# Turned tiles through DRAM: from SyncE's queue to ScalarE's in the input projection

## Chip, cores and metric

One core of a Trainium2 chip. The metric is the device time of one execution in microseconds (us). TensorE multiplies, VectorE (DVE), ScalarE (ACT) and GpSimd (POOL) do the rest, and transfers between SBUF and DRAM are issued by SyncE (SP) or ScalarE, each from its own instruction stream onto its own DMA queue.

## The reference

One layer of a hybrid decoder, for 256 positions and 2048 channels, all in float32:

```
h = rmsnorm(x);  proj = h @ w_in                      # 2048 x 14368
q, k, v, z, b, a, p_in, g_a, g_b = split(proj)
q, k, v = silu(causal_dwconv(q, k, v))                # width 4
o = gated_delta_rule(l2norm(q), l2norm(k), v, g, beta)   # 16 heads of 128
y_a = rmsnorm(o) * silu(z)
y_b = (multi-scale causal pooling of p_in) @ pool_w * pool_scale   # 4 groups
x = x + (sigmoid(g_a) * y_a + sigmoid(g_b) * y_b) @ w_out
gate, up = split(rmsnorm(x) @ w_up)                   # 2 x 5632
x = x + (gelu(causal_dwconv(gate) + bias) * up) @ w_down
return rmsnorm(x)
```

## The kernel before

**Products.** Every weight is read once, in 512 KB tiles of 256 rows by 512 columns. SyncE loads a tile (`raw`, five buffers), ScalarE rounds it to the fast float32 format (`whi`), and VectorE makes the rest (`wlo = raw - whi`). Activations are split in the same way, and each product is three matmuls: eight with `whi` and four with `wlo` for a weight tile, each over 512 columns. The steps `fetch`, `cast` and `split` run ahead of the products, the cast by up to `AHEAD` = 3 tiles. A product leaves positions on partitions and 512 channels along the row.

**Turned tiles.** Convolution, pooling and the next product want channels on partitions. A tile is turned in three steps, in `flip`: VectorE transposes 32 x 32 blocks into `tn`; four DMAs of 128 KB (one for each 32 partitions, in runs of 32 values) write it to DRAM so that the blocks change places (`flip<-tn`); after that has landed one DMA of 512 KB reads it back in rows (`flipped`: `kq<-flip`, `vT<-flip`, `pu<-flip`, `mlo<-flip` in the input projection, `fhl<-flip`, `gs<-flip`, `us<-flip` after it). `flip_back` does the same in the other direction for the values of the delta rule (`back<-tb`, then `vt<-back`).

**Stages.** The input projection runs in four turns (g = 0 to 3) of 512 channels of q, k and v, with the pooling input and gates of the turn before between them. A turn has five flips (keys, queries, values, pooling input, mixed result) and one `flip_back`. Beside the products run the convolutions, the delta rule of four heads (`gdn`, with its own small transfers `cdd`, `lb`, `tbd`, `tct`, `qnd`, `pnt` and the decays `dec`, all on SyncE), pooling (`pooled`) and gates. Then follow the output projection (`residual`, four flips) and the gated MLP (`gated_linear`, `product`, 22 flips), and the down projection.

**Order.** Each engine runs its instructions in the order in which the program writes them. That order is made when the kernel is built: the side work is written as generators (`spawn`), each of which yields the engine that its next piece needs; `side` writes a piece out between two groups of matmuls when a model of the times (`Plan`) says that its inputs are there and its engine isn't too far ahead of TensorE. `Plan.dma` is the model of a transfer: one queue for all of them, 0.42 us of the issuer's time on SyncE and 0.1 us on ScalarE. `pipeline` chooses between `fetch`, `cast` and `split` and goes before the side work of ordinary rank. All five engines' streams follow from the same model, so a change to the model can move any of them.

An instruction that has to wait for a semaphore holds back all that stands behind it in its engine's stream: on SyncE the weight loads, on ScalarE the casts.

Of the kernel before, what the change touches and what calls it, by code (L numbers as in the profile page):

```python
# [13 lines left out]
P = 128  # L14
S = 256
# [16 lines left out]
class Plan:  # L32
# [4 lines left out]
    def __init__(self):  # L37
        self.t = dict(PE=0.0, V=0.0, A=0.0, G=0.0, S=0.0)
        self.ready = self.base = 0.0
        self.queue = 2.5  # L40
        self.table = "s"

    def at(self, time):
# [6 lines left out]
    def dma(self, eng, out):  # L50
        n = 4
        for d in out.shape:
            n *= d
        self.t[eng] = max(self.t[eng], self.base) + (0.42 if eng == "S" else 0.1)
        self.queue = max(self.queue, self.t[eng]) + n / (170e3 if out.shape[-1] <= 32 else 380e3)
        self.ready = max(self.ready, self.queue + 2.0)

    def op(self, eng, name, out, args, kw):
        if name == "dma_start":
# [48 lines left out]
def kernel(  # L108
# [20 lines left out]
    plan = Plan()  # L129
    now = plan.t  # L130
    nc = Engines(plan, tc.nc)
# [12 lines left out]
    def nm(s):  # L144
        cnt[0] += 1
        return f"{s}_{cnt[0]}"
# [32 lines left out]
    def take(*tags):  # L179
        while taken_by(tags):  # L180
            yield
        held.update((tag, 1e9) for tag in tags)
# [7 lines left out]
    def give(*tags):  # L190
        held.update((tag, plan.ready) for tag in tags)
# [25 lines left out]
    def spawn(gen, rank=1):  # L217
        cnt[0] += 1
        threads.append([rank, cnt[0], gen, None, plan.ready])
        follow(threads[-1], next(gen))  # L220
# [152 lines left out]
        return ps  # L373


    def flip(pool, src, of, rank):
        yield "V", -2
        yield from take("tn")
        b = pool.tile([P, 2, 512], F32, tag="tn", name=nm("tn"))
        if of is None:  # L380
            for t in range(2):
                nc.vector.transpose(b[:, t, :], src[:, t, :])
        else:
            nc.vector.transpose(b.rearrange("p t f -> p (t f)"), src.rearrange("p t f -> p (t f)"))
            give(of)
        yield "S"
        d = dpool.tile([512, S], F32, tag="flip", bufs=4, name=nm("flip"))
        dv = d.rearrange("(f i) (t a j) -> a i t f j", i=32, t=2, j=32)
        for a in range(4):
            nc.sync.dma_start(dv[a], b[32 * a : 32 * a + 32].rearrange("p t (f j) -> p t f j", j=32))  # L390
        give("tn")
        yield "S", rank
        return d

    def flipped(dst, d):
        nc.sync.dma_start(dst, d.rearrange("(f p) s -> p f s", p=P))

    def flip_back(pool, src, dst, of):
        yield "V"
        yield from take("tn")  # L400
        b = pool.tile([P, 4, S], F32, tag="tn", name=nm("tb"))
        nc.vector.transpose(b.rearrange("p h s -> p (h s)"), src.rearrange("p h s -> p (h s)"))
        give(of)
        yield "S"
        d = dpool.tile([S, 512], F32, tag="back", name=nm("back"))
        dv = d.rearrange("(n i) (h a j) -> a i h n j", i=32, h=4, j=32)
        for a in range(4):
            nc.sync.dma_start(dv[a], b[32 * a : 32 * a + 32].rearrange("p h (n j) -> p h n j", j=32))
        give("tn")
        yield "S"  # L410
        nc.sync.dma_start(dst.rearrange("p t h d -> p t (h d)"), d.rearrange("(t p) c -> p t c", p=P))

    mix = tc.tile_pool(name="mix", bufs=1)
    mp = mix.__enter__()
# [533 lines left out]

    def pooled(e, g, phi, plo):
        d = yield from flip(mp, e, "ev", g)  # L950
        win = WINDOWS[g]
        spare = g + 5 if g < 3 else 0
        if g == 3:
            yield from take("tn")
        u = mtile(g, [P, 4, S], F32, nm("pu"))
        flipped(u, d)
        yield "V"
        a = mtile(spare, [P, 4, S], F32, nm("pa")) if spare else mp.tile([P, 4, S], F32, tag="tn", name=nm("pa"))
# [105 lines left out]
    for g in range(4):  # L1064
# [5 lines left out]
        def keys(e, g=g, done=done):  # L1070
            d = yield from flip(mp, e, "ev", g)
            yield from take("k", "q")
            kq = mp.tile([P, 4, 2, S], F32, tag="kq", bufs=1, name=nm("kq"))
            done.append(kq)
            yield from conv_silu(d, 1, g, kq[:, :, 0, :])
            done.append(plan.ready)
# [80 lines left out]
    fp = ctx.enter_context(tc.tile_pool(name="ffn", bufs=1))  # L1157
# [13 lines left out]
    def residual(c, ps):  # L1171
        yield "V"
        xs = xt[:, :, c * 512 : (c + 1) * 512]
        if c == 2:
            for t in range(2):
                nc.vector.tensor_tensor(xs[:, t, :], xs[:, t, :], ps[:, t, :], op=ALU.add)
        else:
            nc.vector.tensor_tensor(xs, xs, ps, op=ALU.add)
        spawn(squares(c, xs), 0)
        d = yield from flip(fp, xs, None, 0)  # L1180
        ks = slice(4 * c, 4 * c + 4)
        raw = flo[:, ks, :].bitcast(F32)
        flipped(raw, d)
        for k in range(4 * c, 4 * c + 4):
            if k % 2 == 0:
                yield "A"
            nc.scalar.activation(fhi[:, k, :], raw[:, k - 4 * c, :], AF.Copy, scale=vec[:, V_FFN + k : V_FFN + k + 1])
        for k in range(4 * c, 4 * c + 4):
            if k % 2 == 0:
                yield "V"  # L1190
            nc.vector.scalar_tensor_tensor(flo[:, k, :], raw[:, k - 4 * c, :], vec[:, V_FFN + k : V_FFN + k + 1],
                                           fhi[:, k, :].bitcast(F32), op0=ALU.mult, op1=ALU.subtract)
        high.append(c)

    def squares(c, xs):
        yield "A"
        for t in range(2):
            jk = cpool.tile([P, 512], F32, tag="sqj", name=nm("sqj"))
            nc.scalar.activation(jk, xs[:, t, :], AF.Square, accum_out=ssq4[:, t, c : c + 1])
        squared.append(c)  # L1200
        if len(squared) == 4:
            yield "V"
            nc.vector.tensor_reduce(ssq2, ssq4, axis=mybir.AxisListType.X, op=ALU.add)
            rstd(ssq2, rs2)
            squared.append(4)
# [28 lines left out]
    hlo = []  # L1234

    def gated_linear(c, e, done):
        d = yield from flip(fp, e, "fev", 1)
        yield from take("gs")
        gs = fp.tile([P, 4, S], F32, tag="gs", name=nm("gs"))
        flipped(gs, d)  # L1240
        yield "V"
        yield from take("y")
        y = fp.tile([P, 4, S], F32, tag="y", name=nm("y"))
        for f in range(4):
            yield "V"
            r = 4 * c + f
            nc.vector.tensor_scalar(y[:, f, :], gs[:, f, :], cfw[:, 2 * KF + r : 2 * KF + r + 1],
                                    vec[:, V_CB + r : V_CB + r + 1], op0=ALU.mult, op1=ALU.add)
            for j in (1, 0):
                s = 2 - j  # L1250
                nc.vector.scalar_tensor_tensor(y[:, f, s:], gs[:, f, : S - s], cfw[:, j * KF + r : j * KF + r + 1],
                                               y[:, f, s:], op0=ALU.mult, op1=ALU.add)
        give("gs")
        yield "A"
        nc.scalar.activation(y, y, AF.Gelu)
        done.append((y, plan.ready))

    def product(c, e, hh, hl, done):
        d = yield from flip(fp, e, "fev", 1)
        yield from take("gs")  # L1260
        us = fp.tile([P, 4, S], F32, tag="gs", name=nm("us"))
        flipped(us, d)
        while not done:
            yield
        y, ready = done[0]
        plan.at(max(plan.ready, ready))
        yield "V"
        nc.vector.tensor_tensor(y, us, y, op=ALU.mult)
        give("gs")
        yield "A"  # L1270
        nc.scalar.copy(hh, y)
        yield "V"
        nc.vector.tensor_tensor(hl, y, hh.bitcast(F32), op=ALU.subtract)
        give("y")
# [3 lines left out]
    def up_product(c):  # L1278
        return evicted(gemm_a(fh, fl, KD, range(6, 8), first.pop(0), fh_made) if c == 0 else gemm_a(fh, fl, KD))

    for c in range(DFF // 512):
        e = up_product(c)
        done = []
        spawn(gated_linear(c, e, done))
        e = up_product(c)
        if c < 4:
            hh = mtile(c, [P, 4, S], F32R, f"hhi{c}")
            hl = mtile(4 + c, [P, 4, S], F32R, f"hlo{c}")
        else:
            hh = fp.tile([P, 4, S], F32R, name=f"hhi{c}")  # L1290
            hl = fp.tile([P, 4, S], F32R, name=f"hlo{c}")
        spawn(product(c, e, hh, hl, done))
        hhi.append(hh)
        hlo.append(hl)
# [94 lines left out]
    xs = xt[:, 1, 1536:2048]  # L1389
# [36 lines left out]
```

## Time and profile before

| | |
|---|---|
| time, median of 3 runs | 1534.53 us (1532.87 to 1534.91) |
| the profiled execution | 1536.53 us, its span 1533.5 us |
| TensorE | busy 1519.9 us, 99% of the span |
| VectorE, ScalarE | busy 1059.4 us (69%), 775.4 us (51%) |
| DMA queue of SyncE | 339.32 MB, 75.3% of the 16 DMA engines' time |
| DMA queue of ScalarE | 5.53 MB, 1.1% |

The span is the time from the first to the last instruction. PE is TensorE's matmul stream, PEld its weight loads, and SPq and ACTq are the DMA-issuing instructions of SyncE and ScalarE, which don't count as busy time. Matmul ends are modelled, so a busy TensorE isn't one at its peak; the granted clock (PEclk, 1.00 is full speed) stands beside it. Nearly all instructions have line L94, that of a helper, so groups are told apart by the tiles that they write and read, as `out<-in`. "A <- B" in a list of waits means that A sat idle until B was done; the columns are us in total, times, and the longest. For transfers, "landing" is the time from the issue to the data's arrival.

### The profile page before, as it was taken

How to read it: one execution, taken by the hardware profiler on the slowest of the kernel's cores; microseconds unless marked ns; L12 is line 12 of the kernel's file. 1: busy time of each engine (PE TensorE's matmuls, PEld its weight loads, DVE VectorE, ACT ScalarE, POOL GpSimd, SP SyncE). 2: the span in 40 equal slices, each digit the busy share in tenths (PEclk: the TensorE clock that was granted, in tenths of full speed). 3: DMA queues.
4: the chain of work that ended last, by engine and by line, in shares of the span. 5: the costliest groups of instructions: out<-in, count | busy, mean ns of one | idle time of the engine just before them, and what ended most of it. 6: DMA issues, size and time to landing. Idle time of an engine off the chain costs nothing.

```text
span 1533.5 us, 19655 instructions
## 1 busy us (share of the span) xinstructions
PE 1519.9 (99%) x7110; PEld 1250.0 (82%) x7110; DVE 1059.4 (69%) x1525; ACT 775.4 (51%) x1023; POOL 62.5 (4%) x85
## 2 busy tenths in 40 slices
PE   9999999999999999999999999999999999999997
PEld 8887888777878887888888888888888888888886
DVE  5767878787887779885566766666666666444445
ACT  7475474466545854464455544444454444333343
POOL 1001001100010002000000000000000000000000
PEclk9999999999999999999999999999999999999999
DMA  8888975898578966974798888877887788666663
GB/s 292 224 238 219 256 243 149 206 260 256 159 178 245 288 201 167 264 230 143 228 281 270 235 255 245 258 220 242 253 248 227 237 255 240 204 193 192 220 194 108
DMA packets 399271, 346.09 MB, mean 226 GB/s; under 512 B 231190, under 2 KB 258374, under 8 KB 399174
## 3 DMA queue, kind: packets, MB, share of 16 engines
q1 hardware_dynamic: 395744, 339.32, 75.3%
q10 hardware_dynamic: 3430, 5.53, 1.1%
q8 instruction: 55, 0.90, 0.2%
q14 instruction: 42, 0.34, 0.1%
HBM read 315.40 MB, written 29.39 MB: 225 GB/s over the span
## 4 chain that ended last, share of the span: by engine, by line
PE 93%; DMA 3%; DVE 2%; issue 1%; SPq 0%; ACT 0%; POOLq 0%; POOL 0%; ACTq 0%; DVEq 0%
PE psm L94 79%; PE psa L94 8%; PE psb L94 6%; DMA raw<-in_w_in_dram 2%; DVE wlo L94 1%; DMA lb<-cdd 0%; DMA pu<-flip 0%; SPq L94 0%; DVE tmp L94 0%; ACT whi L94 0%; DVE tb L94 0%; DMA flip<-tn 0%; ACT xt L94 0%; DVE pb L94 0%; DVE tn L94 0%
## 5 line engine op out<-in xcount | busy, mean ns | idle before, releaser
L94 DVE TENSOR_TENSOR wlo<-raw,whi 128x1024 fp32r<-128x1024 f32 x524 | 635.2, 1220 | 293.1 <-ACT whi L94 291.4
L94 ACT CAST whi<-raw 128x1024 fp32r<-128x1024 f32 x526 | 549.0, 1051 | 536.9 <-PE psm L94 360.7
L94 PE MATMUL psm<-whi,xhl 128*128 128x512 f32 x1792 | 452.7, 393 | 1.4 <-ACT whi L94 1.4
L94 PEld LDWEIGHTS psm<-whi,xhl 128*128 128x128 f32 x1792 | 335.4, 188 | 71.6 <-ACT whi L94 2.2
L94 PE MATMUL psm<-whi,fhl 128*128 128x512 f32 x1408 | 347.8, 389 | 0.0
L94 PEld LDWEIGHTS psm<-whi,fhl 128*128 128x128 f32 x1408 | 264.5, 188 | 54.7
L94 PE MATMUL psm<-wlo,xhl 128*128 128x512 f32 x896 | 243.4, 394 | 0.6 <-DVE wlo L94 0.6
L94 PEld LDWEIGHTS psm<-wlo,xhl 128*128 128x128 f32 x896 | 167.4, 188 | 35.6 <-DVE wlo L94 1.1
L94 PE MATMUL psm<-wlo,fhl 128*128 128x512 f32 x704 | 188.3, 389 | 0.0
L94 PEld LDWEIGHTS psm<-wlo,fhl 128*128 128x128 f32 x704 | 132.2, 188 | 27.3
L94 PE MATMUL psm<-whi,hhi 128*128 128x512 f32 x168 | 65.4, 389 | 0.0
L94 PE MATMUL psm<-whi,hlo 128*128 128x512 f32 x168 | 65.4, 389 | 0.0
L94 ACT ACTIVATE fev<-psm,rs 128x512 f32<-128x512 f32 x44 | 27.9, 686 | 55.3 <-PE psm L94 55.3
L94 DVE STREAM_TRANSPOSE tn<-fev 128x1024 f32<-128x1024 f32 x22 | 27.4, 1244 | 32.3 <-ACT fev L94 32.1
L94 DVE SCALAR_TENSOR_TENSOR cy<-kq,cqw,cy 128x255 f32<-128x255 f32 (+2 forms) x96 | 44.5, 481 | 1.6
L94 PE MATMUL psm<-wlo,hhi 128*128 128x512 f32 x168 | 45.2, 389 | 0.0
L94 DVE SCALAR_TENSOR_TENSOR y<-gs,cfw,y 128x255 f32<-128x255 f32 x88 | 42.6, 484 | 3.1
L94 DVE TENSOR_TENSOR tmp<-lb,tb 128x248 f32<-128x248 f32 (+30 forms) x124 | 36.5, 294 | 10.1 <-DMA lb<-cdd 7.3
L94 DVE TENSOR_TENSOR tb<-tb,tmp 128x248 f32<-128x248 f32 (+30 forms) x124 | 36.9, 298 | 4.3
L94 POOL TENSOR_TENSOR rs<-ms,epsx 128x2 f32<-128x2 f32 (+1 forms) x4 | 4.2, 1062 | 822.0 <-DVE ms L94 822.0
L94 PE MATMUL psm<-whi,mhi 128*128 128x512 f32 x96 | 37.4, 389 | 0.0
L94 PE MATMUL psm<-whi,mlo 128*128 128x512 f32 x96 | 37.4, 389 | 0.0
(223 smaller groups left out, 1288.4 us busy)
## 6 DMA issues: line engine op xcount, KB each, us to landing
raw<-in_w_in_dram SPq DMA_DIRECT2D x226, 512.0 KB, 5.3
raw<-in_w_up_dram SPq DMA_DIRECT2D x176, 512.0 KB, 4.5
raw<-in_w_down_dram SPq DMA_DIRECT2D x88, 512.0 KB, 4.6
flip<-tn SPq DMA_DIRECT2D x184, 128.0 KB, 3.2
raw<-in_w_out_dram SPq DMA_DIRECT2D x32, 512.0 KB, 5.1
gs<-flip SPq DMA_DIRECT2D x11, 512.0 KB, 5.5
us<-flip SPq DMA_DIRECT2D x11, 512.0 KB, 6.2
kq<-flip SPq DMA_DIRECT2D x8, 512.0 KB, 8.2
```

Of the source, the lines that this page charges most:

```text
L94: r = getattr(self.eng, op)(out, *args, **kw)
```

## The change

In the input projection the four parts of a turned tile and the read-back are issued by ScalarE in place of SyncE: `flip` and `flip_back` pass their parts to a new generator `sent`, which on ScalarE yields before each of the four, so that other pieces may be written between them. On SyncE (`by="S"`, in `residual`, `gated_linear` and `product`) the four are written together as before. `flipped` takes the issuing engine. Weight loads and the small transfers of the delta rule stay on SyncE. `Plan.dma` has a queue for each of the two issuers, 0.36 us for an issue on ScalarE, and a term for transfers of both queues that share the DMA engines.

```diff
-        self.queue = 2.5
+        self.queue = dict(S=2.5, A=0.0)
...
-        self.t[eng] = max(self.t[eng], self.base) + (0.42 if eng == "S" else 0.1)
-        self.queue = max(self.queue, self.t[eng]) + n / (170e3 if out.shape[-1] <= 32 else 380e3)
-        self.ready = max(self.ready, self.queue + 2.0)
+        self.t[eng] = max(self.t[eng], self.base) + (0.42 if eng == "S" else 0.36)
+
+        other = "A" if eng == "S" else "S"
+        begin = max(self.queue[eng], self.t[eng])
+        took = n / (170e3 if out.shape[-1] <= 32 else 380e3)
+        shared = min(took, max(0.0, self.queue[other] - begin))
+        self.queue[eng] = begin + took + shared
+        self.queue[other] += shared
+        self.ready = max(self.ready, self.queue[eng] + 2.0)
...
-    def flip(pool, src, of, rank):
+    def sent(parts, by="A"):
+        if by == "S":
+            yield "S"
+            for to, src in parts:
+                nc.sync.dma_start(to, src)
+            return
+        at = []
+        for to, src in parts:
+            yield "A"
+            nc.scalar.dma_start(to, src)
+            at.append(plan.ready)
+            plan.at(now["A"])
+        plan.at(max(at))
+
+
+    def flip(pool, src, of, rank, by="A"):
...
-        yield "S"
         d = dpool.tile([512, S], F32, tag="flip", bufs=4, name=nm("flip"))
         dv = d.rearrange("(f i) (t a j) -> a i t f j", i=32, t=2, j=32)
-        for a in range(4):
-            nc.sync.dma_start(dv[a], b[32 * a : 32 * a + 32].rearrange("p t (f j) -> p t f j", j=32))
+        parts = [(dv[a], b[32 * a : 32 * a + 32].rearrange("p t (f j) -> p t f j", j=32)) for a in range(4)]
+        yield from sent(parts, by)
         give("tn")
-        yield "S", rank
+        yield by, rank
         return d
 
-    def flipped(dst, d):
-        nc.sync.dma_start(dst, d.rearrange("(f p) s -> p f s", p=P))
+    def flipped(dst, d, eng=nc.scalar):
+        eng.dma_start(dst, d.rearrange("(f p) s -> p f s", p=P))
...
@@ flip_back
-        yield "S"
...
-        for a in range(4):
-            nc.sync.dma_start(dv[a], b[32 * a : 32 * a + 32].rearrange("p h (n j) -> p h n j", j=32))
+        yield from sent([(dv[a], b[32 * a : 32 * a + 32].rearrange("p h (n j) -> p h n j", j=32)) for a in range(4)])
         give("tn")
-        yield "S"
-        nc.sync.dma_start(dst.rearrange("p t h d -> p t (h d)"), d.rearrange("(t p) c -> p t c", p=P))
+        yield "A"
+        nc.scalar.dma_start(dst.rearrange("p t h d -> p t (h d)"), d.rearrange("(t p) c -> p t c", p=P))
...
@@ residual, and in the same way gated_linear and product
-        d = yield from flip(fp, xs, None, 0)
+        d = yield from flip(fp, xs, None, 0, "S")
-        flipped(raw, d)
+        flipped(raw, d, nc.sync)
```

More of the change, by code (lines that the diff above doesn't have):

```diff
@@ L1236, in gated_linear @@
     def gated_linear(c, e, done):
-        d = yield from flip(fp, e, "fev", 1)
+        d = yield from flip(fp, e, "fev", 1, "S")
         yield from take("gs")
         gs = fp.tile([P, 4, S], F32, tag="gs", name=nm("gs"))
-        flipped(gs, d)
+        flipped(gs, d, nc.sync)
         yield "V"
@@ L1258, in product @@
     def product(c, e, hh, hl, done):
-        d = yield from flip(fp, e, "fev", 1)
+        d = yield from flip(fp, e, "fev", 1, "S")
         yield from take("gs")
         us = fp.tile([P, 4, S], F32, tag="gs", name=nm("us"))
-        flipped(us, d)
+        flipped(us, d, nc.sync)
         while not done:
```

## The prediction

> **What bounds the kernel now.** I read the page first, then the busy time by stretches, then TensorE's waits, then the chain of waits through the only stretch where TensorE stops, and last SyncE's queue in time order.
>
> ```profile
> span 1533.5 us, 19655 instructions
> PE 1519.9 (99%) x7110; PEld 1250.0 (82%) x7110; DVE 1059.4 (69%) x1525; ACT 775.4 (51%) x1023; POOL 62.5 (4%) x85
> ```
>
> TensorE is busy for all but 13.6 us. By stretches (columns: time, then busy us and instructions of each engine, granted clock, DMA share, GB/s):
>
> ```profile
> 35.00:760.00 725.00, 721.93 (x3576) 588.39 (x3575) 566.96 (x972) 393.64 (x583) 53.61 (x60) 1.00 0.77 219
> 760.00:1518.00 758.00, 758.00 (x3346) 628.14 (x3345) 463.38 (x495) 352.31 (x386) 1.81 (x2) 1.00 0.77 230
> ...
> 320.00:340.00 20.00, 19.58 (x87) 15.69 (x86) 17.52 (x40) 14.80 (x34) 1.36 (x2) 1.00 0.99 299
> 340.00:360.00 20.00, 19.37 (x86) 15.70 (x85) 17.70 (x37) 9.77 (x11) 1.85 (x2) 1.00 0.84 252
> ...
> 380.00:400.00 20.00, 17.99 (x112) 14.87 (x111) 16.16 (x28) 8.65 (x13) 0.00 (x0) 0.91 0.64 176
> ```
>
> From 760 us on (output projection and MLP) there is nothing to win. In the input projection, 35 to 760, TensorE is idle for 3.07 us, and the last three rows hold 0.42 + 0.63 + 2.01 = 3.06 of it. In the last row the granted clock is 0.91 besides: 20 x 0.09 = 1.8 us of work lost. So **4.9 us** is all that a change to this projection can win; start and end lie outside it. What TensorE waited for between 320 and 400:
>
> ```profile
> PE psa L94 <- DVE T L94: 2.0, 2, 1.4
> PE psm L94 <- DVE wlo L94: 0.6, 1, 0.6
> PE psm L94 <- ACT whi L94: 0.4, 1, 0.4
> ```
>
> These are split weights that came late (1.0) and a step of the delta rule that came late (2.0). The chain of waits says why:
>
> ```profile
> 298.15 7.59 DMA lb<-cdd
> ...
> 323.29 5.70 DMA raw<-in_w_in_dram
> ...
> 343.24 5.66 DMA raw<-in_w_in_dram
> ...
> 363.05 3.25 DMA flip<-tn
> 366.45 7.59 DMA pu<-flip
> 374.06 1.31 DVE pb L94 x2
> ```
>
> Two weight loads started late; then the read-back `pu<-flip` took 7.59 us, VectorE stood in `pooled` for it, and the delta rule's `T` behind it was late. What stood before them on SyncE's queue (start, time from first to last, number of issues):
>
> ```profile
> 299.94 8.86 SPq L94 DMA_DIRECT2D back<-tb  x4
> ...
> 314.31 8.87 SPq L94 DMA_DIRECT2D flip<-tn  x4
> 323.29 2.50 SPq L94 DMA_DIRECT2D raw<-in_w_in_dram  x4
> ```
>
> For 8.9 us SyncE does nothing but issue four parts of a turned tile, twice within 25 us, and four weight loads come out in a burst behind the second. TensorE uses a tile in 2.7 us (see the lead below), so 8.9 us is more than three tiles.
>
> **The change, part by part.** What is moved in the projection (count; ns min/median/max of one issue):
>
> ```profile
> L94 SPq DMA_DIRECT2D flip<-tn x80: 575/667/3935, 39.8 to 739.9; - x80
> L94 SPq DMA_DIRECT2D kq<-flip x8: 367/367/466, 47.1 to 500.0; - x8
> L94 SPq DMA_DIRECT2D vT<-flip x4: 366/367/565, 92.9 to 525.1; - x4
> L94 SPq DMA_DIRECT2D pu<-flip x4: 367/367/367, 190.8 to 648.6; - x4
> L94 SPq DMA_DIRECT2D mlo<-flip x4: 366/366/367, 276.3 to 743.3; - x4
> DMA to landing us min/median/max: 2.7/4.3/8.9
> ```
> ```profile
> L94 SPq DMA_DIRECT2D back<-tb x16: 575/834/4586, 148.6 to 617.1; - x16
> L94 SPq DMA_DIRECT2D vt<-back x4: 366/367/578, 159.0 to 620.5; - x4
> ```
>
> *1. Removed from SyncE:* 80 x 0.667 + 16 x 0.834 + 24 x 0.367 = 75.5 us of issuing at medians, more with the long ones, and the waits that go with them. What it is worth is read where it ends last: the late `raw` of 320 to 360, 0.42 + 0.63 = 1.05 us. With nothing but weights and small transfers before them these loads go out when their buffers come free. Ends: 0 (the engines, not the queue, hold them: share 0.99 at 320) and -1.05. I take -1.05, since 17.7 us of issuing by SyncE in that stretch is larger than the stall many times over. Next late there is `lb<-cdd` (7.59 us, the first row of the chain), which stays on SyncE.
>
> *2. Read-backs on a queue of their own.* `pu<-flip` left SyncE behind flips and weights and landed 7.59 us later. Alone on ScalarE's queue it has only its own flip ahead. The nearest row is the fastest landing of this group, 2.7 us (rows above); VectorE waited 4.2 us, so landing 4.2 us sooner is enough. Worth 2.01 us of idle time and 1.8 us of clock, which dips right behind that stop: -3.8. Ends 0 and -3.8; I take -3.8.
>
> The Trainium skill's "DMA: Bandwidth & Descriptors", section "Queues, rings and completion order", has each DMA engine take turns between the queues, a packet at a time, so a read-back would pass queued weights and slow them; by this rule part 2 holds, and no stretch here with both queues loaded shows it.
>
> *3. Added to ScalarE.* The same 120 issues, 75.5 us at medians, onto 393.64 us busy in 725: 65% in place of 54%. Do they stop its computing? Its few present issues show:
>
> ```profile
> 32.60 1.05 ACT L94 CAST whi<-raw 128x1024 fp32r<-128x1024 f32 x1 [1.66 <-PE psm L94]
> 32.61 0.33 ACTq L94 DMA_DIRECT2D vrows<-in_norm_ffn_w_dram  x1
> ```
>
> The issue starts 0.01 us after the cast and runs under it: only what is longer than the running instruction delays the next. Queued behind each issue are the weights' casts, for which VectorE's `wlo` and TensorE wait. Their lead is up to three tiles (`AHEAD`); a tile lasts 2.72 us by the `wlo` groups below, so 8.2 us.
>
> ```profile
> 296.05 1.07 PE L94 MATMUL psm<-wlo,xhl 128*128 128x512 f32 x4
> ...
> 298.77 1.07 PE L94 MATMUL psm<-wlo,xhl 128*128 128x512 f32 x4
> ```
>
> The tight stretches are these:
>
> ```profile
> 140.00:160.00 20.00, 20.00 (x90) 16.58 (x89) 14.58 (x25) 16.95 (x38) 1.22 (x2) 1.00 0.99 228
> ...
> 300.00:320.00 20.00, 20.00 (x90) 16.58 (x89) 12.23 (x20) 9.12 (x13) 0.00 (x0) 1.00 0.95 260
> 500.00:540.00 40.00, 40.00 (x244) 32.37 (x243) 31.74 (x53) 32.34 (x64) 1.85 (x2) 1.00 0.95 284
> ```
> ```profile
> 148.60 7.68 SPq L94 DMA_DIRECT2D back<-tb  x4
> ...
> 505.58 3.85 SPq L94 DMA_DIRECT2D back<-tb  x4
> ...
> 514.31 6.76 SPq L94 DMA_DIRECT2D flip<-tn  x4
> ...
> 537.23 3.74 SPq L94 DMA_DIRECT2D flip<-tn  x4
> ```
>
> At medians, with nothing hidden: 140 to 160 has 16.95 + 4 x 0.834 + 2 x 0.367 = 21.0 of 20; 500 to 540 has 32.34 + 4 x 0.834 + 8 x 0.667 + 3 x 0.367 = 42.1 of 40. Overruns of 1.0 and 2.1 us, which the 8.2 us cover. The other end is SyncE's own long durations (rival two). I take **+1.1**, the smaller overrun as if no lead covered it, because an 0.667 us median is nearer to the short end than to 3.9.
>
> *4. Waits that move with them.* From 35 to 790 us SyncE waited (us in total, times, longest):
>
> ```profile
> SPq L94 <- DVE tn L94: 34.6, 19, 6.1
> ...
> SPq L94 <- DMA flip<-tn: 12.0, 21, 2.1
> ```
>
> Now ScalarE waits for the transposed tile and for a flip's landing, with casts queued behind. The longest, 6.1, is under the 8.2 us lead; all together 46.6 us makes 393.64 + 75.5 + 46.6 = 515.7 of 725. Taken as 0, hidden by the lead; if the lead is gone, each costs its own length.
>
> *5. The order.* `Plan.dma` now models two queues and 0.36 us per issue on ScalarE, and `sent` lets other pieces in between the four parts. So every engine's order in the projection is written anew, and pieces may meet elsewhere. Four turns of the same work hold one such stop (4.9 us), which is the size of a new one; the ends are 0 and +4.9. Taken as 0. In the MLP and the residual the issuer stays SyncE; with ScalarE's queue empty there the model gives the same times: 0. SyncE keeps `lb`, `dec`, `tbd`, `tct`, `qnd`, `pnt`; the DMA engines move the same bytes.
>
> **Sum:** -1.05 - 3.8 + 1.1 = -3.75 us. The profiled execution took 1536.5 (3.0 around the span), and would take 1532.8. It lies 2.0 above the median of the runs, 1534.5; against that the forecast is **1530.8**.
>
> **The rivals.**
>
> *One: no change, 1534.5.* The DMA engines are the limit, or the stop only changes place. For it: share 0.99, 0.95 and 0.99 in 140:160, 300:320 and 320:340, so two queues would split the same engines and a weight load would lose what a read-back wins. Parts 1 and 2 become 0, or a stop like today's (+4.9) cancels them. Against it: 380:400 has share 0.64, and the share over the whole projection is 0.77. The Trainium skill, same page, section "Issuing engines are not separate DMA queues", says that more issuing engines "will only save the time on the sequencer it takes to initiate the DMA, which is usually small relative to the DMA itself"; by that rule part 2 would be nothing and the time about 1533.5 at best. A flip part's median issue of 0.667 us against 2.7 to 8.9 us to landing agrees with "usually small", the 3.9 us ones do not.
>
> *Two: slower, 1538.3.* The issues stay as long on ScalarE's queue as on SyncE's, and casts come late. Priced by the rows: 500 to 540, 32.34 + 3.85 + 6.76 + 3.74 + 1.1 = 47.8 of 40, 7.8 over; 140 to 160, 16.95 + 7.68 + 0.73 = 25.4, 5.4 over; 300 to 320, 9.12 + 8.8 + 5.7 (what of the two groups of 8.86 and 8.87 lies in it) = 23.6, 3.6 over. With half the lead there (4.1) the first two cost 3.7 and 1.3; the third, where weights are late already, 3.6: +8.6 in all. With the 4.85 of parts 1 and 2 kept that is 1538.3; with none kept 1543.1. It decides as soon as a group's overrun is larger than the lead; with all 8.2 us there, nothing happens. For it: SyncE's long issues come where the engines are full, and the engines stay the same. Against it: on the new queue no weights or `lb` stand before the parts.
>
> **How the numbers follow.** About 0.2% (3.1 us) can be told from no change. The forecast has 0.50, of which 0.06 falls short of 3.1 us; rival one 0.30, with 0.04 of it slower (a new stop on top); rival two 0.20, with 0.02 within 0.2%. So faster 0.44, same 0.34, slower 0.22. The range: down to 1528.6 (all of 4.9 and 1 us of spread between runs), up to 1538.5, which leaves out about 0.04 below and 0.12 above. The forecast's own range is 1529 to 1532.5.
>
> **What would show it.** Part 1: `raw` issued without a burst behind flips, no TensorE wait for `whi` or `wlo` after 35 us. Part 2: read-backs landing in under 5 us, clock 1.00 in all stretches to 760. Part 3: issues on ScalarE near 0.6 us, casts not waiting for them. Wrong if TensorE waits for `whi` in new places, if issues on ScalarE's queue take 2 us and more, or if weights take much longer than today to land.

## The result, and the profile after

The changed kernel is slower: 1557.74 us median of 6 runs (1551.79 to 1566.39) against 1533.77 us (1532.15 to 1534.91), a ratio of 1.0156, 95% interval 1.0138 to 1.0173. The forecast was 1530.8 with a range to 1538.5. The profiled execution took 1559.34 us, its span is 1557.6.

The page after, its busy times and its DMA queues (packets, MB, share of the 16 engines' time):

```profile
span 1557.6 us, 19700 instructions
PE 1527.8 (98%) x7110; PEld 1251.9 (80%) x7110; DVE 1058.1 (68%) x1525; ACT 775.8 (50%) x1027; POOL 60.9 (4%) x85
...
q1 hardware_dynamic: 284256, 314.14, 67.2%
q10 hardware_dynamic: 114918, 30.70, 8.9%
```

The move took place: 30.70 MB in 114,918 packets now go over ScalarE's queue. Every engine does the same work; the span is 24.1 us longer. TensorE is idle for 29.8 us in place of 13.6, and all of the difference lies in the input projection (columns as in the prediction; the first row holds the whole of it, the others its worst stretches):

```profile
35.00:800.00 765.00, 745.17 (x3645) 603.34 (x3644) 573.79 (x979) 401.04 (x593) 51.99 (x60) 0.99 0.77 215
180.00:200.00 20.00, 17.18 (x68) 13.36 (x67) 16.21 (x29) 12.88 (x25) 0.00 (x0) 0.91 0.80 226
500.00:520.00 20.00, 17.13 (x75) 13.54 (x74) 14.50 (x27) 12.33 (x26) 1.78 (x2) 1.00 0.88 262
560.00:580.00 20.00, 17.20 (x95) 13.10 (x94) 14.88 (x19) 17.85 (x32) 0.00 (x0) 0.91 0.70 213
780.00:800.00 20.00, 15.75 (x58) 12.12 (x57) 9.04 (x9) 6.59 (x7) 0.00 (x0) 0.83 0.85 285
```

From 35 to 800 us TensorE idles for 19.8 us, where it was 3.07. Behind three of the stops the clock dips: 20 x (0.09 + 0.09 + 0.17) = 7.0 us of work lost, where it was 1.8. These two make 16.8 + 5.2 = 22.0 of the 24.1 us. TensorE's waits over the whole span after:

```profile
PE psm L100 <- ACT whi L100: 9.7, 8, 1.9
PE psm L100 <- ACT mhi L100: 3.8, 1, 3.8
PE psa L100 <- ACT T L100: 2.7, 2, 2.1
PE psb L100 <- DVE bat L100: 1.7, 1, 1.7
PE psa L100 <- DVE ga L100: 1.4, 3, 0.9
```

ScalarE ends the longest: it is late with casts (9.7 us in eight stops), with the last turn's mixed tile (`mhi`) and with the delta rule's `T`. ScalarE itself is busy for half of the time, as it was before. Its stream in time order at one of the stops, with its DMA issues (ACTq):

```profile
174.77 1.05 ACT L100 CAST whi<-raw 128x1024 fp32r<-128x1024 f32 x1
174.80 3.68 ACTq L100 DMA_DIRECT2D flip<-tn  x3
178.57 1.05 ACT L100 CAST whi<-raw 128x1024 fp32r<-128x1024 f32 x1 [2.76 <-DMA flip<-tn]
178.65 4.30 ACTq L100 DMA_DIRECT2D vt<-back  x1
183.00 1.71 ACT L100 ACTIVATE cy<-kq,cqw 128x256 f32<-128x256 f32 x4 [3.38 <-issue]
184.62 1.03 ACT L100 CAST whi<-raw 128x1024 fp32r<-128x1024 f32 x1
```

The first issue does start under the running cast, as the prediction said. But 3.68 and 4.30 us of issuing don't fit under 1.05 us each. The 4.30 us are a single read-back, whose like take 0.38 us at the median: it comes right behind four parts. So from 174.77 to 184.62 ScalarE makes two casts where TensorE uses more than three tiles (2.7 us each).

### The profile page after: what moved, and what is told of

It is laid out like the page before. It is cut to its first block, busy times and chain, and to the rows that moved or that the text cites. A ratio compares the mean times of both kernels' runs of the same rounds, so it can differ in the third digit from the quotient of the medians.

```text
span 1557.6 us, 19700 instructions
## 1 busy us (share of the span) xinstructions
PE 1527.8 (98%) x7110; PEld 1251.9 (80%) x7110; DVE 1058.1 (68%) x1525; ACT 775.8 (50%) x1027; POOL 60.9 (4%) x85
## 3 DMA queue, kind: packets, MB, share of 16 engines
q10 hardware_dynamic: 114918, 30.70, 8.9%
## 4 chain that ended last, share of the span: by engine, by line
PE 85%; DMA 6%; ACTq 2%; ACT 2%; DVE 2%; issue 2%; POOL 0%; POOLq 0%; SPq 0%; DVEq 0%
PE psm L100 73%; PE psa L100 7%; PE psb L100 5%; ACTq L100 2%; DMA flip<-tn 2%; DMA raw<-in_w_in_dram 1%; DMA back<-tb 1%; ACT whi L100 1%; DMA mlo<-flip 1%; DVE wlo L100 1%; DMA kq<-flip 1%; DMA dec<-rund 0%; PE psa L459 0%; DMA pu<-flip 0%; DVE tb L100 0%
## 5 line engine op out<-in xcount | busy, mean ns | idle before, releaser
L100 PEld LDWEIGHTS psm<-wlo,hhi 128*128 128x128 f32 x168 | 31.5, 188 | 6.6
```

Source lines behind the costliest of these rows:

```text
L100: r = getattr(self.eng, op)(out, *args, **kw)
```

## The experiments

The expectations name theories. W: ScalarE stands in its own stream for transfers to land, with casts behind. I, later S: the sum of the issues costs the time. O: the new order alone does. Q: two parts fill the queue, and the third and fourth stand in ScalarE's stream until it drains. E: two loaded queues share the DMA engines, so that all lands later. Each ratio is to the kernel before, run beside it.

**The model alone.** The kernel before with the whole new `Plan.dma` and no other line of the change; the turned tiles are issued by SyncE.

```diff
+        self.queue = dict(S=2.5, A=0.0)
...
+        self.t[eng] = max(self.t[eng], self.base) + (0.42 if eng == "S" else 0.36)
...
```

> Everything is issued by SyncE as before; only the new Plan.dma (two queues, 0.36 us) is there, so every engine's order is the new model's. Theory W (ScalarE stands in its own stream for transfers to land, in front of the casts): 1532 to 1537, as before. Theory I (the 110 us of issuing hold ScalarE up): the same, 1532 to 1537. Theory O (the new order alone makes pieces meet badly): 1550 or more.

1529.43 us, 0.9962 (0.9947 to 0.9977): faster than the kernel before, and O falls. The stop at 320 to 400 is gone:

```profile
35.00:760.00 725.00, 725.00 (x3601) 591.97 (x3600) 569.39 (x974) 398.86 (x587) 52.58 (x60) 1.00 0.78 221
```

TensorE doesn't idle once from 35 to 760 us. Yet SyncE's queue still carries the same long issues, and the read-back lands as late as before (issues of both; for the read-back the landing too, one of four on record, as min/median/max):

```profile
L100 SPq DMA_DIRECT2D flip<-tn x92: 581/668/4068, 38.8 to 797.2; - x92
...
L100 SPq DMA_DIRECT2D pu<-flip x4: 366/366/367, 190.3 to 647.0; - x4
DMA to landing us min/median/max: 7.6/7.6/7.6
```

So neither SyncE's long issues nor a read-back of 7.6 us was enough for that stop; it came from how pieces met in that order.

**Only the parts on ScalarE**, read-backs back on SyncE:

```diff
-        yield by, rank
+        yield "S", rank
...
-    def flipped(dst, d, eng=nc.scalar):
+    def flipped(dst, d, eng=nc.sync):
...
-        yield "A"
-        nc.scalar.dma_start(dst.rearrange("p t h d -> p t (h d)"), d.rearrange("(t p) c -> p t c", p=P))
+        yield "S"
+        nc.sync.dma_start(dst.rearrange("p t h d -> p t (h d)"), d.rearrange("(t p) c -> p t c", p=P))
```

> The four parts stay on ScalarE, the read-back is issued by SyncE again. 97 of the 110 us of issuing stay on ScalarE, the waits for a flip's landing leave it. Theory W: most of the 24 us is gone, 1536 to 1543. Theory I: the loss stays, 1552 to 1558. Theory O: not told apart, the order is near the changed kernel's, 1550 or more.

1555.46 us, 1.0133 (1.0117 to 1.0148): nearly the whole loss, so W is not its main part. ScalarE's stream and TensorE's wait at the longest stop:

```profile
498.33 1.05 ACT L100 CAST whi<-raw 128x1024 fp32r<-128x1024 f32 x1 [2.78 <-DVE wlo L100]
498.41 10.68 ACTq L100 DMA_DIRECT2D flip<-tn  x4
509.14 1.70 ACT L100 ACTIVATE cy<-kq,cqw 128x256 f32<-128x256 f32 x4 [9.76 <-DMA flip<-tn]
510.75 2.92 ACT L100 CAST whi<-raw 128x1024 fp32r<-128x1024 f32 x3
```
```profile
PE psm L100 <- ACT whi L100: 4.9, 1, 4.9
```
```profile
500.00:520.00 20.00, 15.08 (x55) 11.90 (x54) 10.80 (x23) 10.83 (x23) 1.22 (x2) 0.83 0.82 254
```

Four parts hold ScalarE's stream for 10.68 us and no cast starts from 498.33 to 510.75, 12.4 us. The lead of three tiles is 8.2 us; TensorE stops for 4.9 and the clock dips behind it.

**Only the read-backs on ScalarE**, parts back on SyncE (in `flip_back` alike):

```diff
-        yield from sent(parts, by)
+        yield from sent(parts, "S")
...
```

> The four parts go back to SyncE, the read-back stays on ScalarE. Only 13 us of issuing stay on ScalarE, with the waits for a flip's landing. Theory W: most of the loss stays, 1547 to 1557, and ScalarE's waits for flip and back stay in its list. Theory I: as before, 1532 to 1537.

1531.78 us, 0.9981 (0.9972 to 0.9991): no loss. Waits for landing in ScalarE's stream, with short issues, are covered.

**A later landing in the model:**

```diff
-        self.ready = max(self.ready, self.queue[eng] + 2.0)
+        self.ready = max(self.ready, self.queue[eng] + (2.0 if eng == "S" else 5.0))
```

> The changed kernel, but the model has a transfer of ScalarE's queue land 3 us later (5.0 for 2.0), as the trace has it (flips 5.5 us from issue to landing), so read-backs and their readers are written later into the order. The issues stay the same. Theory W, with a model that is too early as its reason: under half of the loss is left, 1535 to 1545. Theory I: unchanged, 1553 to 1560.

1547.81 us, 1.0088 (1.0067 to 1.0110), between both expectations. Later read-backs help by some 10 us, but stops for casts stay (14.0 us in five). This order differs in other ways too, so it doesn't price the waits.

How long one issue takes depends on its place among the four. Each issue of a flip part in the projection, in ns (min/median/max, worked out from the single issues of each trace):

```
kernel                        1st            2nd            3rd             4th
before (SyncE)            575/576/689   627/664/3935   667/1398/3686   666/696/1372
after (ScalarE)           577/577/682   577/680/692    577/1258/2866   680/962/3117
only the parts (ScalarE)  577/577/695   670/684/1327   577/1434/6334   679/2222/3676
```

On ScalarE's queue the first two go in quickly nearly always; the third and fourth are the long ones. They don't wait for SyncE to finish issuing: in the middle of the longest, 6.33 us from 499.85 in the run with only the parts moved, SyncE issued a weight load on its own queue in 0.37 us (at 501.14), and 9 of the 25 issues over 1.5 us of that run meet no issue of SyncE at all. In the changed kernel's order 22 of 24 groups have no cast between the second and the third. That is theory Q, and the next runs try it.

**A gap after the second part**, so that a cast is written there:

```diff
             at.append(plan.ready)
-            plan.at(now["A"])
+            plan.at(now["A"] + (2.0 if len(at) == 2 else 0.0))
```

> The changed kernel, but after the second of the four parts the model holds the third back for 2 us, so that a weight cast is written between them in all 24 turns (2 of 24 before). Issues, bytes and queues stay the same. Theory Q (two parts fill the queue, the third and fourth stand in ScalarE's stream until it drains, with the casts behind them): long issues (over 1.5 us) mostly gone, 1533 to 1545. Theory S (the sum of the issues on ScalarE costs the time): 1552 to 1560. Theory E (two loaded queues share the DMA engines, and everything lands later): 1552 to 1560.

1540.09 us, 1.0034 (1.0023 to 1.0046): 18 of the 24 us are back. S and E fall. One point of Q's expectation missed: 15 issues are still over 1.5 us, as many as in the changed kernel. It isn't the long issue by itself that costs, but how many stand together ahead of a cast. What is left is one stop:

```profile
PE psm L100 <- ACT mhi L100: 7.3, 1, 7.3
...
PE psm L100 <- ACT whi L100: 0.9, 1, 0.9
```

It is the output projection's wait for the last turn's mixed tile, whose last part was issued at 756.4 us here (775.8 in the changed kernel, 739.9 before). That this is the 2 us gap in the last flip was not tried.

**The same order, other rows.** The projection's parts are written in 4 KB rows (in `flip_back` alike):

```diff
-        dv = d.rearrange("(f i) (t a j) -> a i t f j", i=32, t=2, j=32)
+        dv = d.rearrange("(a i x) s -> a i (x s)", a=4, i=32)
...
```

> The changed kernel with its order, issues and bytes, but the projection's 96 parts are written to DRAM in rows of 4 KB, not in runs of 128 bytes, so the data isn't turned there (the blocks don't change places). Theory Q: an issue falls to under 0.5 us, none is long, and the time to 1529 to 1538. Theory S: an issue's price doesn't hang on the rows, 1550 or more. An order that is bad by itself: 1545 or more.

1531.93 us, 0.9985 (0.9975 to 0.9995).

```profile
L100 ACTq DMA_DIRECT2D flip<-tn x80: 308/434/737, 38.7 to 750.8; - x80
```

With the order of the changed kernel, the same 120 issues by ScalarE and the same bytes, the loss is gone once the longest issue of a part is 0.77 us (in `flip_back`) in place of 3.12. So neither the order nor ScalarE's issuing as such costs anything: the 128-byte runs do. The flips' parts also land sooner here, 3.6 us after the issue where it was 5.5; this run can't tell that from the shorter issues, but the last one below can.

**Another order for the kernel before:**

```diff
-        self.t[eng] = max(self.t[eng], self.base) + (0.42 if eng == "S" else 0.1)
+        self.t[eng] = max(self.t[eng], self.base) + (0.37 if eng == "S" else 0.1)
```

> The kernel before with one number of its model changed (0.37 us for 0.42 per issue of SyncE): the work is the same, the order differs in places. If the stop at 320 to 390 us of the kernel before is an accident of order: 1529 to 1533, or a stop elsewhere. If it belongs to the work: 1533 to 1536.

1532.36 us, 0.9984 (0.9975 to 0.9993), inside what can't be told from no change. The granted clock doesn't dip between the start and the end of this run; its waits for split weights are 2.7 us. It points the way of the first run and is too small to show it.

**The parts on GpSimd's queue**, read-backs on SyncE:

```diff
-            yield "A"
-            nc.scalar.dma_start(to, src)
+            yield "G"
+            nc.gpsimd.dma_start(to, src)
```

> The four parts are issued by GpSimd, read-backs by SyncE: a queue apart from the weights', but nothing of it in ScalarE's stream. Theory Q and theory S: 1529 to 1540, if GpSimd's issues are not much longer than ScalarE's. Theory E: 1545 or more.

1529.48 us, 0.9963 (0.9950 to 0.9976).

```profile
L101 POOL DMA_DIRECT2D flip<-tn x80: 814/814/1047, 38.8 to 738.5; - x80
...
DMA to landing us min/median/max: 3.5/5.7/7.2
```

The same parts on a queue apart from the weights', 5.7 us to landing, and no loss: landing that late costs nothing by itself. The run doesn't settle E alone, though. The trace has the parts on GpSimd's queue as 32 packets of 4 KB each (and 16 of 4 bytes), where ScalarE's queue has 1,024 of 128 bytes, so more than the issuer changed:

```profile
q0 software_dynamic: 4608, 12.59, 3.8%
```

**Two parts on ScalarE, two on SyncE**, read-backs on SyncE:

```diff
-        for to, src in parts:
-            yield "A"
-            nc.scalar.dma_start(to, src)
+        for n, (to, src) in enumerate(parts):
+            yield "A" if n < 2 else "S"
+            (nc.scalar if n < 2 else nc.sync).dma_start(to, src)
...
```

> As the run with the parts on ScalarE and read-backs on SyncE, but only the first two of the four parts are issued by ScalarE, the other two by SyncE. Theory Q (the first two parts always go in, the third and fourth stand until the queue drains): no issue of ScalarE over 1 us, no long stop behind it, 1529 to 1537. Theory S (the sum of the issues on ScalarE): about half of that run's 20 us is left, 1543 to 1547.

1529.46 us, 0.9968 (0.9957 to 0.9980). Two of four parts on ScalarE cost nothing, where all four cost 20 us:

```profile
L100 ACTq DMA_DIRECT2D flip<-tn x40: 577/597/1093, 38.4 to 747.2; - x40
L100 SPq DMA_DIRECT2D flip<-tn x40: 575/792/3557, 39.9 to 747.2; - x40
```

So the cost doesn't grow with the sum; it sets in when more parts follow each other, as Q has it (two issues of ScalarE are a little over the 1 us that Q named, 1.01 and 1.09). The long issues are SyncE's now, up to 3.56 us, and there they cost nothing. E is out as well: the packets are those of the changed kernel, both queues are loaded, and ScalarE's parts land after 5.1 us, about as late as the 5.5 there. What costs is that the long issues stand in the stream of the engine that casts. How much the queue holds was not measured by itself; that two parts fill it is read from these runs.

Three versions end at 1529.4 to 1529.5: the model alone, GpSimd and two and two. In all of them TensorE has hardly a stop left between start and end, so little is left to win in this stage. They beat the kernel before by about 0.35%; the simplest is the new model with all issues on SyncE.

## Why the prediction was wrong

**The bound was about right.** 4.9 us was said to be all that can be won, and the best versions win 4.9 to 5.8 (1 - 0.9968 and 1 - 0.9962 of 1534). What failed is a term of the sum.

**Step 3 failed.** It put +1.1 us on issuing by ScalarE; with the parts alone moved this cost 20.4 us (1555.46 against 1535.04 beside it). It priced 120 issues at medians, 75.5 us (they took 110.0: 78.4 for flips, 18.5 for `back<-tb`, 13.1 for read-backs), and covered each group's overrun with 8.2 us of lead. Two things were mis-sized. The third and fourth issues are as long on ScalarE's queue as on SyncE's: the 80 flip parts sum to 78.4 us there and 82.0 before, because it is their own 128-byte runs, not weights ahead of them, that make an issue long (in 4 KB rows on ScalarE's queue none is over 0.77 us). And an average over 20 or 40 us hides what counts, the longest stretch without a cast: 12.4 us in the run with only the parts moved, 10.7 of them four issues in a row, against a lead of 8.2. That lead is no sharp limit: with the parts in 4 KB rows 10.2 us once passed between the starts of two casts (from 158 us), and TensorE didn't stop. The row with a 0.33 us issue under a cast showed an issue of another kind, a small load.

**Rival two was the mechanism, and its price was too low.** It said that issues stay as long and that it decides when a group exceeds the lead, gave it 0.20, and priced it at +8.6 us less 4.85. Of the measured 24.0 us it missed the stops outside the three stretches that it priced (the largest at 46, 184 to 190, 489, 565 and 785 us; of the 19.8 us of idle time only 4.3 lie inside them), the clock dips (+5.2 us) and the work that waits for ScalarE further on (`T`, `mhi`).

**Step 4 held alone, not in company.** Waits for landing cost nothing where the parts are on SyncE (the run with read-backs only). In the changed kernel they add to it in places:

```profile
539.92 0.37 ACTq L100 DMA_DIRECT2D vT<-flip  x1
540.40 2.94 ACT L100 CAST whi<-raw 128x1024 fp32r<-128x1024 f32 x3 [8.08 <-PE psm L100]
```

ScalarE's stream stood before `vT<-flip` for 6.9 us until the flip had landed, and the casts came 8.08 us after the last; the `PE psm` named there had been done long before.

**Steps 1 and 2 gave the right sum by luck.** The 4.9 us came back with SyncE issuing everything, so they were not the worth of an emptier queue or of a faster read-back. Two rows were misread besides. The 2.7 us that step 2 took as the nearest landing belong to a part of 128 KB; the read-backs `kq<-flip` on record there took 4.4 to 8.9. And of the 17.7 us that step 1 counted as issuing between 320 and 360, all but 3.2 lie before 320, and 2.6 are a wait between two parts. In the changed kernel some read-backs did land sooner:

```profile
kq<-flip ACTq DMA_DIRECT2D x8, 512.0 KB, 6.2
...
vT<-flip ACTq DMA_DIRECT2D x4, 512.0 KB, 5.0
```

against 8.2 and 8.7 us before (medians of the landings on record, four of eight and one of four; `vt<-back` took 8.3, 7.7 before). But a queue of their own isn't what did it. With only the read-backs on ScalarE's queue these two took 8.4 and 5.4 us, and `pu<-flip` 9.2; with the parts on GpSimd's queue and the read-backs on SyncE's, among the weights, both took 4.1. What makes a read-back land sooner stays open; few landings are on record. The weights of `w_in` land in 4.5 us, 5.3 before, so they were not slowed. The Trainium skill's "DMA: Bandwidth & Descriptors", section "Queues, rings and completion order", lets a read-back pass queued weights; no run here shows that, and the sooner landings moved no end.

**Step 5** named the order as an unknown with ends 0 and +4.9 and took 0; it was -5.6 by the model-only run, outside those ends, since a new order can also undo an old stop.

**Rival one** took the DMA engines for the limit. They weren't: the DMA share of the projection is 0.77 before and after, and the run with the model alone lost all its stops there with the same bytes. The Trainium skill's sentence in "DMA: Bandwidth & Descriptors", section "Issuing engines are not separate DMA queues", that more issuing engines only save the sequencer's time, fits: with the parts taken off SyncE, the GpSimd run won nothing over the model-only run. On ScalarE that time isn't small: 6.33 us at the longest, with the casts behind it in the same stream.

## What to carry to other kernels

Before a transfer goes to a computing engine's queue, look at the longest single issue and at how many stand in a row, not at the median: an issue that isn't taken at once holds the engine's whole stream (6.33 us for one part here), and what counts is the longest stretch without the work that others wait for, set against that work's lead. Transfers in many short runs belong on an engine that has nothing urgent behind them, or at most as many in a row as go in at once (two parts here). And where a model writes the order, run the model's change without the move: here it alone was worth 5.6 us, and in the versions with GpSimd and with two and two it would have been credited to the move.

## What was not expected of the hardware

An issue's price depends on the runs: 128 KB in 128-byte runs takes 0.58 to 0.68 us for the first two, the same bytes in 4 KB rows 0.43 at the median, and the longest are 6.33 and 0.77 us. GpSimd's issues of the flips' parts took 0.814 us at the median and 1.05 at most, without any long one, and the trace shows them in packets of 4 KB. And some stops are followed by a clock dip that makes them dearer, 1.8 us of work in the kernel before and 7.0 in the changed one. The length of a stop alone doesn't decide it: one of 1.2 us (at 46.9 us, only the parts moved) was followed by a dip, one of 2.0 us (at 504.5, only the read-backs moved) wasn't.
